# Attention with one shift row, 64-row keys for the maxima, a closing norm on VectorE and output weights loaded two ahead

## The chip, the core and the metric

The kernel runs on one core of a Trainium2 chip. The time is the device time of one execution in microseconds. The engines are TensorE (PE in the profile, its weight loads PEld), VectorE (DVE), ScalarE (ACT), GpSimd (POOL) and SyncE (SP), which here only issues transfers. Each engine takes its instructions in a fixed order and waits at the front of its queue for whatever the next one needs.

## What is computed

One layer on a sequence of 2048 positions of width 1024, cut to its steps:

```python
h = layer_norm(x) * (1 + scale) + shift               # scale, shift, gate = silu(c) @ w_ada + b_ada
xr, zr, q, k, v, za, fl = split(h @ w_in)
y_r = rms_norm(rg_lru(conv(xr))) * silu(zr)           # recurrent half, width 512
d = cumsum(log_sigmoid(fl + b_fgate))                 # one decay per head and position
s = q @ k.T * 64**-0.5 + d[query] - d[key]            # 8 heads of 64, causal
y_a = rms_norm(softmax(s) @ v) * silu(za)             # attention half, width 512
y = concat(y_r, y_a) @ w_out
out = layer_norm(2**0.25 * x + gate * y) * ln_gain + ln_bias
```

Each fp32 operand of the large products is split into a high and a low fp16 part, and a product is three matmuls (high by high, high by low, low by high).

## The kernel before

Up to about 590 us of the span the kernel computes the norm, the projections, the recurrence and the keys, and the sum of the output gate (`gate_gen`, seven GpSimd additions of 1024 columns, line 957). What follows is one long attention stage of 32 units: four query chunks `ci` of 512 positions by eight heads `h`. A unit has two parts.

`maxpass` runs ahead of its unit. It loads the keys `kk` of the head: plane 0 holds the high part in rows 0 to 63 and the low part in rows 64 to 127, from the DRAM tensor `kd`; plane 1 holds the high part again and four further rows, from a second DRAM tensor `kb` of 68 rows (two rows of the constant 1024, two rows with the decay of the keys). It multiplies the high part of the queries `qb` by plane 1 into PSUM (`pmx`, 68 rows), and VectorE takes row maxima (`mc`, line 1259). From the maximum of a query and its decay comes the shift that is subtracted from the scores. Three VectorE instructions on 128x4 elements (lines 1267 to 1269) write it as a high and a low fp16 column into `z`; four small matmuls (`pzt`) transpose `z`, and ScalarE copies two rows into rows 64 and 65 of `qb`.

The unit's steps follow, one for each block of 128 keys. `s_t` makes the scores by two matmuls into `pst`: plane 0 by both parts of the queries (`qs`), and the first 66 rows of plane 1 by `qb`, which brings in the shift. ScalarE takes the exponential (`pf32`) and casts it to the high part (`ph`, line 1292); the low part is a subtraction, on GpSimd for three blocks of four (line 1294) and on VectorE for the fourth (line 1296). `av` follows five steps later and multiplies both parts by the values `V` into `acc`; `fin` divides by the sum and collects the heads in `Y`. The scores, the maxima and the transposes of the shift share five PSUM banks.

Between the steps runs side work, a few yields at a time: the queries of later chunks (`q_side`), the output weights (`wout_gen`) and, from the first finished chunk on, the output (`out_gen`). `wout_gen` loads each of eight weight blocks `woraw` (128x1024) one block ahead, multiplies it by the gate `gbc` on GpSimd (line 1003) right after the load is issued, and splits it. These blocks, the gate, the keys of the first two chunks and the residual tiles `xres` share one pool of eight buffers (`r4`). `out_gen` multiplies each tile of 128 positions by the weights in two halves of 512 columns (48 matmuls), adds the residual `xres` (line 1468), and hands it to `ln_gen`: statistics on VectorE, the reciprocal root `rs` on GpSimd (line 1395), then a small VectorE instruction for `nm`, one ScalarE instruction over 1024 columns (line 1385), and two GpSimd instructions over 1024 columns with the gain and the bias (lines 1387 and 1388). The last tile has a form of its own, `out_last`, with four VectorE instructions of 512 columns (lines 1427 and 1429).

The program is written as generators; the tool that builds it then settles the order on each engine by its own estimate of times. So an edit at one place moves instructions elsewhere as well.

Of the kernel before, what the change touches and what calls it, by code (L numbers as in the profile page):

```python
# [10 lines left out]
F16 = mybir.dt.float16  # L11
# [8 lines left out]
P = 128  # L20
# [18 lines left out]
def hybrid_mixer(  # L39
# [34 lines left out]
    def cst(shape, name, dt=F32):  # L74
        return con.tile(shape, dt, name=name, tag=name)
# [10 lines left out]
    def sm(shape, name, dt=F32):  # L86
        return sb.tile(shape, dt, name=name, tag="sm", bufs=24)
# [15 lines left out]
            tick()  # L103

    kd = dr.tile([H, P, S], F16, name="kd", tag="kd")
    kb = dr.tile([H, 68, S], F16, name="kb", tag="kb")
    vd = dr.tile([S, C], F32, name="vd", tag="vd")
    qd = dr.tile([H, P, S], F16, name="qd", tag="qd")
    zd = dr.tile([4, P, S], F32, name="zd", tag="zd")
# [755 lines left out]
    nc.vector.tensor_scalar(L8p, sp, 8.0, None, ALU.mult)  # L865
    crow = r4([2, S], "crow", F16)
    nc.vector.memset(crow, RS)
    nc.scalar.dma_start(kb[:, DH:DH + 2, :].rearrange("h a s -> a h s"), crow.unsqueeze(1).broadcast_to([2, H, S]))
    QB = [cst([68, CH], f"qb{i}", F16) for i in range(4)]
    Z = [cst([P, 4, 68], f"Z{i}", F16) for i in range(4)]  # L870
    for q in QB:
        nc.scalar.dma_start(q[66:68, :], crow[:, 0:CH])
    for z in Z:
        nc.gpsimd.memset(z, 0.0)

# [7 lines left out]
    def qk_store(dsts, p, hl, sl):  # L883
        for e in range(2):
            es = slice(e * DH, (e + 1) * DH)
            for dst, lo_i, hi_i in dsts:
                nc.sync.dma_start(dst[2 * p + e, hi_i * DH:(hi_i + 1) * DH, sl], hl[es, 0])
                if lo_i is not None:
                    nc.sync.dma_start(dst[2 * p + e, lo_i * DH:(lo_i + 1) * DH, sl], hl[es, 1])

    k_sc = []

    def k_fin(p, u, sts, cols):
        yield
        yield
        am = yield from all_max(col_max(cols))
        inv, rec = sm([P, 1], "ki"), sm([P, 1], "kr")
        scales(am, 4.0, inv, rec)
        f = cst([P, 1], f"fk{p}")
        nc.vector.tensor_tensor(f, u, inv, ALU.mult)  # L900
        k_sc.append(f)
        yield
        for half in range(2):
            hl = wh([P, 2, D], "khl")
            split_out(hl[:, 0], hl[:, 1], sts[half].rearrange("p a b -> p (a b)"), rec)
            qk_store([(kd, 1, 0), (kb, None, 0)], p, hl, slice(half * D, (half + 1) * D))
            yield

    def k_group(p):
# [32 lines left out]
    def gate_gen():  # L942
        for k in range(KT):
            raw = r4([P, D], "woraw")
            nc.sync.dma_start(raw, w_out_v[k])
            nc.vector.tensor_reduce(out=wocol[:, k:k + 1], in_=raw, axis=AX.X, op=ALU.max, apply_absolute_value=True)
            if k % 2 == 1:
                yield
        acc = None
        for k in range(KT):  # L950
            w = r4([P, D], "wgate")
            nc.sync.dma_start(w, w_ada_v[k, :, 2 * D:3 * D])
            nc.scalar.activation(w, w, AF.Copy, scale=cact[:, k:k + 1])
            if acc is None:
                acc = w
            else:
                nc.gpsimd.tensor_tensor(out=acc, in0=acc, in1=w, op=ALU.add)
            if k % 2 == 1:
                yield
        gbc = r4([P, D], "gbc")  # L960
        nc.sync.dma_start(gbc, b_ada[0, 2 * D:3 * D].partition_broadcast(P))
        for n in range(2):
            sl = slice(n * CH, (n + 1) * CH)
            ps = bank("C", "pgt")
            mm(ps, ones, acc[:, sl], True, True)
            nc.vector.tensor_tensor(gbc[:, sl], ps, gbc[:, sl], ALU.add)
        gate["bc"] = gbc
        yield
        cols = sm([P, 2], "amg")
        col_max(g_col, AX.X, cols[:, 0:1])  # L970
        col_max(gbc, AX.X, cols[:, 1:2])
        chains.append(gate_fin(cols))
        yield
# [10 lines left out]
    def wout_gen():  # L984
        gbc = gate["bc"]
        wm = sm([P, KT], "wm")
        nc.vector.tensor_tensor(wm, wocol, mk, ALU.mult)
        col = col_max(wm)
        yield
        yield  # L990
        am = yield from all_max(col)
        am_w = sm([P, 1], "am_w")
        nc.vector.tensor_scalar(am_w, am, TINY, gate["am"], ALU.max, ALU.mult)
        scales(am_w, RS, sc_o[:, 1:2], sc_o[:, 0:1])
        nc.vector.tensor_scalar(kap, sc_o[:, 1:2], 1.0 / YT, None, ALU.mult)
        so = cst([P, KT], "so")
        nc.vector.tensor_tensor(so, g_col, mk, ALU.mult)
        nc.vector.tensor_scalar(so, so, sc_o[:, 0:1], 1.0 / ALPHA, ALU.mult, ALU.mult)
        yield
        def wo_raw(k):  # L1000
            raw = r4([P, D], "woraw")
            nc.sync.dma_start(raw, w_out_v[k])
            nc.gpsimd.tensor_tensor(out=raw, in0=raw, in1=gbc, op=ALU.mult)
            return raw

        nxt = wo_raw(0)
        yield
        for k in range(KT):
            raw = nxt
            if k + 1 < KT:  # L1010
                nxt = wo_raw(k + 1)
            w = wh([P, 2, D], "wo") if k < KT - 1 else r4([P, 2, D], "wo", F16)
            for n in range(2):
                sl = slice(n * CH, (n + 1) * CH)
                split_out(w[:, 0, sl], w[:, 1, sl], raw[:, sl], so[:, k:k + 1])
                yield
            wo.append(w)

# [66 lines left out]
    def decay_gen():  # L1085
# [37 lines left out]
        nc.vector.tensor_tensor(ndr[:, 1], ndf, ndr[:, 0], ALU.subtract)  # L1123
        for h in range(H):
            for a in range(2):
                nc.sync.dma_start(kb[h, DH + 2 + a, :].rearrange("(t p) -> t p", p=P), ndr[h * TT:(h + 1) * TT, a, :])
        yield

    dg = decay_gen()
# [101 lines left out]
    def maxpass(ci, h, res):  # L1231
        n = cnt[0]
        cnt[0] += 1
        qb, z = QB[n % 4], Z[n % 4]
        sl = slice(ci * CH, (ci + 1) * CH)
        nk = (ci + 1) * CH
        if ci < 2:
            kk = r4([P, 2, 2 * CH], "kk", F16)
        else:
            kk = sb.tile([P, 2, S], F16, name="kk", tag="H", bufs=8)  # L1240
        nc.sync.dma_start(kk[:, 0, 0:nk], kd[h, :, 0:nk])
        nc.sync.dma_start(kk[0:68, 1, 0:nk], kb[h, :, 0:nk])
        nc.sync.dma_start(qb[0:DH, :], qd[h, DH:P, sl])
        qs = sb.tile([P, CH], F16, name="qs", tag="qs", bufs=3)
        nc.sync.dma_start(qs, qd[h, :, sl])
        nc.gpsimd.memset(qb[DH:DH + 2, :], 0.0)
        res.append((kk, qb, qs))
        yield
        mc = sm([P, 4, 4], "mc")
        for i in range(4):  # L1250
            nk = (4 * ci + i + 1) * P
            for b in range(ci + 1):
                w = min(CH, nk - b * CH)
# [5 lines left out]
                nc.vector.tensor_reduce(out=mc[:, i, b:b + 1], in_=ps[:, 0:w], axis=AX.X, op=ALU.max)  # L1259
                yield  # L1260
        if ci > 0:
            m = sm([P, 4], "mrow")
            nc.vector.tensor_reduce(out=m, in_=mc[:, :, 0:ci + 1], axis=AX.X, op=ALU.max)
        else:
            m = mc[:, :, 0]
        t = sm([P, 4], "trow")
        nc.vector.tensor_scalar(t, m, -1.0 / RS, ndc[:, ci, h:h + 1], ALU.mult, ALU.add)  # L1267
        nc.vector.tensor_copy(z[:, :, DH], t)  # L1268
        nc.vector.tensor_tensor(z[:, :, DH + 1], t, z[:, :, DH], ALU.subtract)  # L1269
        yield True  # L1270
        yield True
        with tc.issue_after(last["pe"]):
            ps = bank("A", "pzt")
            for i in range(4):
                mm(ps[0:DH + 2, i * P:(i + 1) * P], z[:, i, 0:DH + 2], ident16, i == 0, i == 3, True)
        yield
        nc.scalar.copy(qb[DH:DH + 2, :], ps[DH:DH + 2, :])

    def s_t(ci, h, kt, kk, qb, qs):
        q0 = max(0, kt - 4 * ci) * P  # L1280
# [2 lines left out]
        ps = bank("A", "pst")  # L1283
        mm(ps[:, 0:w], kk[:, 0, ks], qs[:, q0:CH], True, False)
        md = kt >= 4 * ci
        mm(ps[:, 0:w], kk[0:DH + 2, 1, ks], qb[0:DH + 2, q0:CH], False, not md)
        if md:
            mm(ps[:, 0:P], maskn, identb, False, True)
        pf32 = t2([P, CH], "pf32")
# [84 lines left out]
    def ln_gen(tt, xt):  # L1374
# [9 lines left out]
        nc.vector.scalar_tensor_tensor(nm, mv[:, 0:1], -1.0, rs, ALU.mult, ALU.mult)
        nc.scalar.activation(xt, xt, AF.Identity, scale=rs, bias=nm)  # L1385
        yield
        nc.gpsimd.tensor_tensor(out=xt, in0=xt, in1=late["lng"], op=ALU.mult)
        nc.gpsimd.tensor_tensor(out=xt, in0=xt, in1=late["lnb"], op=ALU.add)
# [230 lines left out]
```

## Time and profile before

| quantity | value |
|---|---|
| median of 3 runs | 1217.73 us (1213.55 to 1219.83) |
| profiled execution, time | 1211.64 us |
| its span in the profile | 1209.9 us |
| TensorE busy | 1111.2 us (92%) |
| VectorE / ScalarE / GpSimd busy | 767.7 / 719.6 / 686.0 us |
| mean granted clock of TensorE | 0.966 |

In the profile's views a line names the engine, the source line, the operation and the tiles, with the result left of the arrow. `L93` is the helper that records every matmul, so matmuls are told apart by their tiles. A wait reads "engine line <- what it waited for: us in total, times, longest". In the views by window each engine has busy us and, in brackets, the number of instructions; the granted clock is a share of full speed. "SPq" is the issue of a transfer, not the transfer itself.

### The profile page before, as it was taken

Reading aid. Unit: us, or ns where it says so; the run is one execution under the profiler, and the core shown is the slowest. Engines: PE = TensorE matmul, PEld = TensorE weight load, DVE = VectorE, ACT = ScalarE, POOL = GpSimd, SP = SyncE. Lnnn points to the kernel's source line nnn. Section 1 sums busy time; section 2 is a strip of 40 time slices with the busy share of each in tenths; the row PEclk is TensorE's granted clock in tenths of the full one; section 3 lists DMA queues with packets and bytes.
Section 4 is the critical chain, followed back from the end, with each engine's and each line's share of the span. In section 5 each row is a group of like instructions: output and inputs, shape, how many; then the busy total and the mean of one; then the engine's idle time right before and its main releaser. Section 6 shows DMA issues by size and latency. Waiting matters only on the chain. (4 is left out here: it accounts for less than half of the span.)

```text
span 1209.9 us, 20217 instructions
## 1 busy us (share of the span) xinstructions
PE 1111.2 (92%) x7467; PEld 622.8 (51%) x7467; DVE 767.7 (63%) x1435; ACT 719.6 (59%) x1244; POOL 686.0 (57%) x670
## 2 busy tenths in 40 slices
PE   6997899999999899999979979989999989999787
PEld 6874444454444444434445545555565555565444
DVE  4378775766668953664396544576677677667534
ACT  3437545564758412623375657577888688888841
POOL 5715532444554300830277645687788689887854
PEclk9998989999999999999979989989999999999899
DMA  9653046221225712754063344222332233221001
GB/s 296 208 151 123 1 118 189 71 64 33 70 70 141 242 55 70 260 160 140 26 205 114 95 129 123 87 93 86 101 94 90 76 103 106 78 89 46 18 27 70
DMA packets 110248, 130.56 MB, mean 108 GB/s; under 512 B 10086, under 2 KB 79318, under 8 KB 110150
## 3 DMA queue, kind: packets, MB, share of 16 engines
q1 hardware_dynamic: 109840, 129.17, 35.0%
q8 instruction: 58, 0.95, 0.3%
q14 instruction: 40, 0.33, 0.1%
q10 hardware_dynamic: 310, 0.12, 0.0%
HBM read 97.66 MB, written 31.59 MB: 107 GB/s over the span
## 5 line engine op out<-in xcount | busy, mean ns | idle before, releaser
L93 PE MATMUL pj<-hT,wT 128*128 128x512 f16 x1440 | 324.4, 383 | 4.1 <-DVE hT L347 1.7
L1294 POOL TENSOR_TENSOR ph<-pf,ph 128x512 f16<-128x512 f32 (+2 forms) x240 | 260.5, 1100 | 67.4 <-ACT ph L1292 62.6
L93 PEld LDWEIGHTS <-wT 128*128 128x128 f16 x1792 | 169.2, 99 | 208.6 <-issue 21.6
L1259 DVE TENSOR_REDUCE mc<-pmx 128x1 f32<-128x512 f32 (+2 forms) x320 | 184.8, 603 | 114.2 <-PE pmx L93 110.0
L1290 ACT ACTIVATE pf<-pst,bias 128x512 f32<-128x512 f32 (+1 forms) x320 | 194.7, 634 | 66.4 <-PE pst L93 58.8
L1292 ACT CAST ph<-pf 128x512 f16<-128x512 f32 (+1 forms) x320 | 171.7, 569 | 20.1 <-PE acc L93 15.9
L93 PE MATMUL acc<-V,ph 128*128 128x129 f16 (+1 forms) x2176 | 158.6, 210 | 22.0 <-POOL ph L1294 14.6
L93 PEld LDWEIGHTS <-ph 128*128 128x128 f16 x2176 | 124.1, 99 | 80.6 <-POOL ph L1294 22.1
L93 PE MATMUL pst<-qs,kk 128*128 128x512 f16 (+1 forms) x320 | 114.3, 360 | 2.0 <-DVE mc L1259 1.3
L93 PE MATMUL pst<-qb,kk 66*128 66x512 f16 (+1 forms) x320 | 112.8, 362 | 0.2
L93 PE MATMUL pmx<-kk,qb 68*128 68x512 f16 (+2 forms) x320 | 105.0, 357 | 7.4 <-DMA kk<-kb 3.8
L93 PE MATMUL pout<-wo,yT 128*128 128x512 f16 (+1 forms) x396 | 95.7, 372 | 1.5 <-ACT yT L1370 1.5
L93 PE MATMUL pout<-wo,yr 128*128 128x512 f16 (+1 forms) x396 | 94.1, 381 | 2.8 <-DVE zs L1369 2.7
L93 PE MATMUL pj<-wN,hT 128*128 128x512 f16 x384 | 89.5, 378 | 0.2 <-ACT XL L814 0.2
L1188 POOL TENSOR_TENSOR XL<-XL,szr 128x512 f32<-128x512 f32 x16 | 24.3, 1522 | 114.7 <-ACT szr L1185 114.7
L1296 DVE TENSOR_TENSOR ph<-pf,ph 128x512 f16<-128x512 f32 (+1 forms) x80 | 64.3, 804 | 33.8 <-ACT ph L1292 33.2
L93 PEld LDWEIGHTS <-kk 66*128 66x128 f16 (+1 forms) x640 | 55.1, 100 | 34.5 <-issue 11.6
L93 PE MATMUL pq<-hT,wT 128*128 128x512 f16 x288 | 67.0, 379 | 2.8 <-DVE qhl L881 2.8
L93 PEld LDWEIGHTS <-hT 128*128 128x128 f16 x640 | 44.5, 97 | 48.3 <-issue 3.6
L93 PEld LDWEIGHTS <-yr 128*128 128x128 f16 x396 | 38.3, 100 | 42.8 <-issue 8.0
L93 PEld LDWEIGHTS <-yT 128*128 128x128 f16 x396 | 37.5, 98 | 39.4 <-ACT yT L1370 1.7
L483 POOL TENSOR_TENSOR xl<-xc,xh 128x512 fp32r<-128x512 f32 x16 | 24.4, 1532 | 57.8 <-ACT xh L481 47.0
(307 smaller groups left out, 1846.0 us busy)
## 6 DMA issues: line engine op xcount, KB each, us to landing
wraw<-in_w_in_dram SPq DMA_DIRECT2D x40, 512.0 KB
woraw<-in_w_out_dram SPq DMA_DIRECT2D x16, 512.0 KB
xres<-in_x_dram SPq DMA_DIRECT2D x16, 512.0 KB
out_dram<-xres SPq DMA_DIRECT2D x15, 512.0 KB
wadab<-in_w_ada_dram SPq DMA_DIRECT2D x8, 512.0 KB
xt<-in_x_dram SPq DMA_DIRECT2D x16, 256.0 KB
xt<-in_x_dram SPq DMA_DIRECT2D x8, 512.0 KB
wsh<-in_w_ada_dram SPq DMA_DIRECT2D x16, 256.0 KB
```

Source lines behind the costliest of these rows:

```text
L93: m = nc.tensor.matmul(o, lhsT=l, rhs=r, start=st, stop=sp, skip_group_check=chk)
L483: nc.gpsimd.tensor_tensor(out=xl, in0=xc, in1=xh, op=ALU.subtract)
L1188: nc.gpsimd.tensor_tensor(out=XL[j][:, sl], in0=XL[j][:, sl], in1=sz, op=ALU.mult)
L1259: nc.vector.tensor_reduce(out=mc[:, i, b:b + 1], in_=ps[:, 0:w], axis=AX.X, op=ALU.max)
L1290: nc.scalar.activation(pf32[:, 0:w], ps[:, 0:w], AF.Exp, scale=DH ** -0.5, bias=bias[:, ci, h, kt:kt + 1])
L1292: nc.scalar.copy(ph[:, 0, 0:w], pf32[:, 0:w])
L1294: nc.gpsimd.tensor_tensor(out=ph[:, 1, 0:w], in0=pf32[:, 0:w], in1=ph[:, 0, 0:w], op=ALU.subtract)
L1296: nc.vector.tensor_tensor(ph[:, 1, 0:w], pf32[:, 0:w], ph[:, 0, 0:w], ALU.subtract)
```

## The change

It has four parts. The shift becomes one fp16 column and one row (one VectorE instruction instead of three). The second DRAM copy of the keys' high part goes: plane 1 takes its 64 rows from `kd` again and three rows from a `kb` that holds only one constant row and the two rows of the decay. The gate's sums and the products of the output weights run on GpSimd in halves of 512 columns; the weights are loaded two blocks ahead, and their product is issued a block ahead of the split. The closing norm of the first 15 tiles takes the form of the last one: four VectorE instructions of 512 columns, and none on ScalarE or on GpSimd after `rs`.

```diff
@@ stores and loads of the keys
-    kb = dr.tile([H, 68, S], F16, name="kb", tag="kb")
+    kb = dr.tile([H, 3, S], F16, name="kb", tag="kb")
...
-    nc.scalar.dma_start(kb[:, DH:DH + 2, :].rearrange("h a s -> a h s"), crow.unsqueeze(1).broadcast_to([2, H, S]))
-    QB = [cst([68, CH], f"qb{i}", F16) for i in range(4)]
+    nc.scalar.dma_start(kb[:, 0:1, :].rearrange("h a s -> a h s"), crow[0:1].unsqueeze(1).broadcast_to([1, H, S]))
+    QB = [cst([67, CH], f"qb{i}", F16) for i in range(4)]
...
-        nc.scalar.dma_start(q[66:68, :], crow[:, 0:CH])
+        nc.scalar.dma_start(q[65:67, :], crow[:, 0:CH])
...
-            qk_store([(kd, 1, 0), (kb, None, 0)], p, hl, slice(half * D, (half + 1) * D))
+            qk_store([(kd, 1, 0)], p, hl, slice(half * D, (half + 1) * D))
...
-                nc.sync.dma_start(kb[h, DH + 2 + a, :].rearrange("(t p) -> t p", p=P), ndr[h * TT:(h + 1) * TT, a, :])
+                nc.sync.dma_start(kb[h, 1 + a, :].rearrange("(t p) -> t p", p=P), ndr[h * TT:(h + 1) * TT, a, :])
...
         nc.sync.dma_start(kk[:, 0, 0:nk], kd[h, :, 0:nk])
-        nc.sync.dma_start(kk[0:68, 1, 0:nk], kb[h, :, 0:nk])
+        nc.sync.dma_start(kk[0:DH, 1, 0:nk], kd[h, 0:DH, 0:nk])
+        nc.sync.dma_start(kk[DH:DH + 3, 1, 0:nk], kb[h, :, 0:nk])
@@ sum of the gate
-                nc.gpsimd.tensor_tensor(out=acc, in0=acc, in1=w, op=ALU.add)
+                for n in range(2):
+                    sl = slice(n * CH, (n + 1) * CH)
+                    nc.gpsimd.tensor_tensor(out=acc[:, sl], in0=acc[:, sl], in1=w[:, sl], op=ALU.add)
@@ output weights
         def wo_raw(k):
             raw = r4([P, D], "woraw")
             nc.sync.dma_start(raw, w_out_v[k])
-            nc.gpsimd.tensor_tensor(out=raw, in0=raw, in1=gbc, op=ALU.mult)
             return raw
 
-        nxt = wo_raw(0)
-        yield
+        def wo_gate(raw):
+            for n in range(2):
+                sl = slice(n * CH, (n + 1) * CH)
+                nc.gpsimd.tensor_tensor(out=raw[:, sl], in0=raw[:, sl], in1=gbc[:, sl], op=ALU.mult)
+
+        raws = [wo_raw(0), wo_raw(1)]
+        yield
+        wo_gate(raws[0])
         for k in range(KT):
-            raw = nxt
-            if k + 1 < KT:
-                nxt = wo_raw(k + 1)
+            raw = raws.pop(0)
             w = wh([P, 2, D], "wo") if k < KT - 1 else r4([P, 2, D], "wo", F16)
             for n in range(2):
                 sl = slice(n * CH, (n + 1) * CH)
                 split_out(w[:, 0, sl], w[:, 1, sl], raw[:, sl], so[:, k:k + 1])
+                if n == 0 and k + 2 < KT:
+                    raws.append(wo_raw(k + 2))
+                if n == 0 and k + 1 < KT:
+                    wo_gate(raws[0])
                 yield
@@ maxima and shift
-        nc.gpsimd.memset(qb[DH:DH + 2, :], 0.0)
+        nc.gpsimd.memset(qb[DH:DH + 1, :], 0.0)
...
-                mm(ps[:, 0:w], qb[:, i * P:(i + 1) * P], kk[0:68, 1, b * CH:b * CH + w], True, not end)
+                mm(ps[:, 0:w], qb[:, i * P:(i + 1) * P], kk[0:67, 1, b * CH:b * CH + w], True, not end)
...
-        t = sm([P, 4], "trow")
-        nc.vector.tensor_scalar(t, m, -1.0 / RS, ndc[:, ci, h:h + 1], ALU.mult, ALU.add)
-        nc.vector.tensor_copy(z[:, :, DH], t)
-        nc.vector.tensor_tensor(z[:, :, DH + 1], t, z[:, :, DH], ALU.subtract)
+        nc.vector.tensor_scalar(z[:, :, DH], m, -1.0 / RS, ndc[:, ci, h:h + 1], ALU.mult, ALU.add)
...
-                mm(ps[0:DH + 2, i * P:(i + 1) * P], z[:, i, 0:DH + 2], ident16, i == 0, i == 3, True)
-        yield
-        nc.scalar.copy(qb[DH:DH + 2, :], ps[DH:DH + 2, :])
+                mm(ps[0:DH + 1, i * P:(i + 1) * P], z[:, i, 0:DH + 1], ident16, i == 0, i == 3, True)
+        yield
+        nc.scalar.copy(qb[DH:DH + 1, :], ps[DH:DH + 1, :])
...
-        mm(ps[:, 0:w], kk[0:DH + 2, 1, ks], qb[0:DH + 2, q0:CH], False, not md)
+        mm(ps[:, 0:w], kk[0:DH + 1, 1, ks], qb[0:DH + 1, q0:CH], False, not md)
@@ closing norm, ln_gen
-        nm = sm([P, 1], "nm")
-        nc.vector.scalar_tensor_tensor(nm, mv[:, 0:1], -1.0, rs, ALU.mult, ALU.mult)
-        nc.scalar.activation(xt, xt, AF.Identity, scale=rs, bias=nm)
-        yield
-        nc.gpsimd.tensor_tensor(out=xt, in0=xt, in1=late["lng"], op=ALU.mult)
-        nc.gpsimd.tensor_tensor(out=xt, in0=xt, in1=late["lnb"], op=ALU.add)
+        for n in range(2):
+            ns = slice(n * CH, (n + 1) * CH)
+            nc.vector.scalar_tensor_tensor(xt[:, ns], xt[:, ns], mv[:, 0:1], late["lng"][:, ns], ALU.subtract, ALU.mult)
+            yield
+        for n in range(2):
+            ns = slice(n * CH, (n + 1) * CH)
+            nc.vector.scalar_tensor_tensor(xt[:, ns], xt[:, ns], rs, late["lnb"][:, ns], ALU.mult, ALU.add)
+            if n == 0:
+                yield
```

The order on the engines moves as follows. SP, where the last of the eight weight blocks is loaded (`kk` are keys, `yr` the recurrent half, `qd` the stored queries); before:

```order
L1242 DMA kk_6507<-kb_64 68x1024
L1245 DMA qs_6511<-qd_66 128x512
L1243 DMA qb0_1604<-qd_66 64x512
L1241 DMA kk_7814<-kd_63 128x1536
L887 DMA qd_66<-qhl_6548 64x512 x2
L889 DMA qd_66<-qhl_6548 64x512 x2
L1242 DMA kk_7814<-kb_64 68x1536
L1241 DMA kk_8101<-kd_63 128x1536
L1242 DMA kk_8101<-kb_64 68x1536
L1326 DMA yr_8216<-yd_68 128x2x512 x4
L1245 DMA qs_6784<-qd_66 128x512
L1002 DMA woraw_6555<-in_w_out_dram 128x1024
```

and now:

```order
L887 DMA qd_66<-qhl_6369 64x512
L888 DMA qd_66<-qhl_6369 64x512
L1003 DMA woraw_6379<-in_w_out_dram 128x1024
L1252 DMA qb0_1604<-qd_66 64x512
L1249 DMA kk_6485<-kd_63 128x1024
L1250 DMA kk_6485<-kd_63 64x1024
L1251 DMA kk_6485<-kb_64 3x1024
L1249 DMA kk_7780<-kd_63 128x1536
L1250 DMA kk_7780<-kd_63 64x1536
L1251 DMA kk_7780<-kb_64 3x1536
```

The last `woraw` stood behind the key loads of two later units and the four of `yr`; now it stands ahead of them, and a key load has three rows.

GpSimd at the product of this block (`ph` the low part of the probabilities, `ytmp` and `Y` the collection of a finished head); before:

```order
L1294 TENSOR_TENSOR ph_6533<-pf32_6531,ph_6533 128x512
L1316 TENSOR_TENSOR ytmp_6633<-ytmp_6633 128x2x64
L1294 TENSOR_TENSOR ph_6566<-pf32_6564,ph_6566 128x512
L1317 TENSOR_TENSOR Y_6236<-ytmp_6633,rv_6635 128x2x64
L1294 TENSOR_TENSOR ph_6622<-pf32_6620,ph_6622 128x512
L1294 TENSOR_TENSOR ph_6654<-pf32_6652,ph_6654 128x384
L1246 MEMSET qb1_1605 2x512
L1003 TENSOR_TENSOR woraw_6555<-woraw_6555,gbc_4622 128x1024
L1294 TENSOR_TENSOR ph_6694<-pf32_6692,ph_6694 128x256
```

and now:

```order
L1300 TENSOR_TENSOR ph_6474<-pf32_6472,ph_6474 128x512
L1009 TENSOR_TENSOR woraw_6379<-woraw_6379,gbc_4613 128x512 x2
L1322 TENSOR_TENSOR ytmp_6605<-ytmp_6605 128x2x64
L1322 TENSOR_TENSOR ytmp_6611<-ytmp_6611 128x2x64
L1340 TENSOR_TENSOR yrst_6497<-yss_6366,mhalf_91 128x4
L1323 TENSOR_TENSOR Y_6216<-ytmp_6605,rv_6607 128x2x64
L1323 TENSOR_TENSOR Y_6216<-ytmp_6611,rv_6613 128x2x64
L1300 TENSOR_TENSOR ph_6512<-pf32_6510,ph_6512 128x512
L1300 TENSOR_TENSOR ph_6544<-pf32_6542,ph_6544 128x512
L1300 TENSOR_TENSOR ph_6600<-pf32_6598,ph_6600 128x512
```

The product came after the subtractions that are now named ph_6512 to ph_6632; it now comes ahead of them, as two halves.

VectorE at the shift of one unit; before:

```order
L1296 TENSOR_TENSOR ph_9833<-pf32_9831,ph_9833 128x512
L1263 TENSOR_REDUCE mrow_9868<-mc_9662 128x4
L1267 TENSOR_SCALAR trow_9870<-mrow_9868,ndc_3534 128x4
L1268 CAST Z2_1610<-trow_9870 128x4
L1269 TENSOR_TENSOR Z2_1610<-trow_9870,Z2_1610 128x4
L1259 TENSOR_REDUCE mc_9968<-pmx_9969 128x1
```

and now:

```order
L1302 TENSOR_TENSOR ph_9782<-pf32_9780,ph_9782 128x512
L1272 TENSOR_REDUCE mrow_9817<-mc_9612 128x4
L1275 TENSOR_SCALAR Z2_1610<-mrow_9817,ndc_3522 128x4
L1477 SCALAR_TENSOR_TENSOR xres_9054<-pout_9751,kap_1622,xres_9054 128x512
L1384 BN_STATS bst_9692<-xres_9054 128x6
```

Two of the three small instructions are gone, and the transfer needs only the one that is left.

VectorE a little further on, at the closing norm of a tile; before:

```order
L1380 BN_AGGR mv_10003<-bst_9743 128x2
L1296 TENSOR_TENSOR ph_9932<-pf32_9930,ph_9932 128x128
L1393 TENSOR_SCALAR ve_10005<-mv_10003 128x1
L1314 RECIPROCAL rv_10064<-ytmp_10062 128x2
L1259 TENSOR_REDUCE mc_9968<-pmx_9988 128x1
L1259 TENSOR_REDUCE mc_9968<-pmx_9991 128x1
L1468 SCALAR_TENSOR_TENSOR xres_9609<-pout_10045,kap_1622,xres_9609 128x512
L1259 TENSOR_REDUCE mc_9968<-pmx_10023 128x1
L1259 TENSOR_REDUCE mc_9968<-pmx_10038 128x1
L1314 RECIPROCAL rv_10070<-ytmp_10068 128x2
L1259 TENSOR_REDUCE mc_9968<-pmx_10041 128x1
L1384 SCALAR_TENSOR_TENSOR nm_10123<-mv_10003,rs_10007 128x1
```

and now:

```order
L1268 TENSOR_REDUCE mc_9917<-pmx_9918 128x1
L1386 BN_AGGR mv_9952<-bst_9692 128x2
L1302 TENSOR_TENSOR ph_9880<-pf32_9878,ph_9880 128x128
L1402 TENSOR_SCALAR ve_9954<-mv_9952 128x1
L1391 SCALAR_TENSOR_TENSOR xres_9054<-xres_9054,mv_9952,lng_7040 128x512 x2
L1395 SCALAR_TENSOR_TENSOR xres_9054<-xres_9054,rs_9956,lnb_7042 128x512 x2
L1268 TENSOR_REDUCE mc_9917<-pmx_9937 128x1
L1268 TENSOR_REDUCE mc_9917<-pmx_9940 128x1
```

Where one small `nm` came nine instructions behind `ve`, four instructions of 512 columns now follow `ve` directly, the last two of them behind `rs` from GpSimd; the maxima `mc` of the next unit stand behind them.

More of the change, by code (lines that the diff above doesn't have):

```diff
@@ L887, in qk_store @@
                 nc.sync.dma_start(dst[2 * p + e, hi_i * DH:(hi_i + 1) * DH, sl], hl[es, 0])
-                if lo_i is not None:
-                    nc.sync.dma_start(dst[2 * p + e, lo_i * DH:(lo_i + 1) * DH, sl], hl[es, 1])
+                nc.sync.dma_start(dst[2 * p + e, lo_i * DH:(lo_i + 1) * DH, sl], hl[es, 1])
     k_sc = []
```

## The prediction

> **What bounds the kernel now.** I read the engine shares of the page first, then busy time by stage, then the waits of the attention stage, and last the places where TensorE stands longest.
>
> The share of TensorE over the span:
>
> ```profile
> PE 1111.2 (92%) x7467; PEld 622.8 (51%) x7467; DVE 767.7 (63%) x1435; ACT 719.6 (59%) x1244; POOL 686.0 (57%) x670
> ```
>
> TensorE is the bound. The change takes no matmul away, so it can only shorten the 99 us in which TensorE is idle (1209.9 - 1111.2) and the stretches in which its clock is lowered. By stage (columns: length; busy us and instructions of PE, PEld, DVE, ACT, POOL; granted clock; DMA share; GB/s):
>
> ```profile
> 590.00:800.00 210.00, 184.62 (x1451) 106.91 (x1449) 129.79 (x286) 140.20 (x288) 136.12 (x163) 0.94 0.40 118
> 800.00:1000.00 200.00, 187.91 (x1600) 109.07 (x1601) 140.34 (x264) 153.28 (x299) 154.84 (x163) 0.96 0.29 92
> 1000.00:1160.00 160.00, 149.55 (x1373) 89.63 (x1371) 103.43 (x184) 132.43 (x253) 135.65 (x130) 0.97 0.19 65
> 1160.00:1210.00 50.00, 40.99 (x220) 21.52 (x218) 19.48 (x40) 9.30 (x13) 22.30 (x15) 0.95 0.14 52
> ```
>
> The edits lie almost wholly in these four stages, which hold 57 us of the idle time (620 - 563.1). From 800 to 1160 ScalarE (286 of 360 us) and GpSimd (290) are fuller than VectorE (244). What TensorE and the two others wait for between 590 and 1210 us (total us, times, longest):
>
> ```profile
> PE acc L93 <- POOL ph L1294: 14.6, 20, 3.5
> PE pzt L93 <- DVE Z L1269: 9.1, 10, 2.3
> ...
> PE pmx L93 <- DMA kk<-kb: 3.8, 3, 1.5
> ...
> PE pmx L93 <- DVE mc L1259: 2.3, 4, 1.6
> ...
> PE pst L93 <- DVE mc L1259: 1.3, 4, 0.7
> ```
>
> ```profile
> DVE mc L1259 <- PE pmx L93: 108.0, 90, 7.6
> ```
>
> ```profile
> POOL ph L1294 <- ACT ph L1292: 62.6, 45, 8.9
> ...
> POOL woraw L1003 <- DMA woraw<-in_w_out_dram: 14.3, 5, 7.6
> ```
>
> Two waits of TensorE are aimed at by the change: for the small parts of the probabilities (GpSimd), and for the shift (VectorE). VectorE itself mostly waits for TensorE, so it has room.
>
> **Output weights two ahead.** Eight 512 KB loads keep their number; each is now issued two blocks early, and the multiply by the gate one block early, in halves. The worst place before:
>
> ```profile
> 679.62 0.54 SPq L1241 DMA_DIRECT2D kk<-kd  x1
> ...
> 696.38 1.49 SPq L1002 DMA_DIRECT2D woraw<-in_w_out_dram  x1
> ...
> 704.27 2.34 POOL L1003 TENSOR_TENSOR woraw<-woraw,gbc 128x1024 f32<-128x1024 f32 x1 [7.65 <-DMA woraw<-in_w_out_dram]
> ```
>
> ```profile
> 700.00:710.00 10.00, 4.83 (x28) 2.36 (x27) 2.61 (x3) 4.49 (x10) 5.73 (x5) 0.84 0.36 109
> 710.00:720.00 10.00, 9.06 (x46) 4.77 (x46) 7.27 (x13) 5.68 (x11) 5.51 (x7) 0.65 0.39 126
> ```
>
> GpSimd stood 7.65 us before a multiply whose weights had been asked for 7.9 us earlier, and the probabilities queued behind it. In these 20 us TensorE was idle 5.17 + 0.94 = 6.1 us, and at the lowered clock it lost at most 1.6 + 3.5 = 5.1 us more (slice times one minus the clock). So the gain is 11.2 us at most. In the new order this load stands on SP ahead of the keys that were issued from 679.62 on, so some 17 us sooner, while its multiply stands only four subtractions sooner on GpSimd. The other end is a loss: three raw blocks instead of two share eight buffers with the keys, and late keys already cost the 3.8 us of the waits above. I take -8, nearer the gain, because the load gets 17 us of lead and the multiply gives back only some 5 (four subtractions of 1.1 us, whose row stands below).
>
> **Shift as one row.** Per unit (32 of them) three instructions on VectorE become one; the transfer matmuls and the copy keep their number:
>
> ```profile
> L1267 DVE TENSOR_SCALAR trow<-mrow,ndc 128x4 f32<-128x4 f32 x24 | 14.7, 614 | 0.7
> L1268 DVE CAST Z<-trow 128x4 f16<-128x4 f32 x32 | 14.5, 454 | 0.5
> L1269 DVE TENSOR_TENSOR Z<-trow,Z 128x4 f16<-128x4 f32 x32 | 18.4, 574 | 0.9
> ```
>
> ```profile
> L1267 DVE TENSOR_SCALAR trow<-mrow,ndc x24: 219/530/1174, 652.3 to 1128.6; 128x4 f32<-128x4 f32 x24
> L1268 DVE CAST Z<-trow x32: 164/178/1134, 590.3 to 1129.8; 128x4 f16<-128x4 f32 x32
> ```
>
> The new instruction is not in the trace. It has the arithmetic of L1267 and the output of L1268, so it lies between 164 and 1174 ns; I take L1267's 614, its nearest relative. VectorE saves 32 x (454 + 574) = 32.9 us. On the path this counts only where the transfer waits, at most 9.1 us. Why four columns can take 2 us:
>
> ```profile
> 936.96 2.36 POOL L1388 TENSOR_TENSOR xres<-xres,lnb 128x1024 f32<-128x1024 f32 x1
> 937.08 2.27 DVE L1269 TENSOR_TENSOR Z<-trow,Z 128x4 f16<-128x4 f32 x1
> 939.41 0.64 PE L93 MATMUL pzt<-ident,Z 128*66 128x128 f16 x4 [1.64 <-DVE Z L1269]
> ```
>
> The little subtraction ends when GpSimd's 1024-column addition ends, and TensorE stands behind it. Of 1.64 us a unit (614 + 454 + 574) 63% goes, so 63% of 9.1 is 5.7; I take -5, ends 0 and -9.1. After such waits the clock falls:
>
> ```profile
> 800.00:810.00 10.00, 8.65 (x46) 4.63 (x47) 7.64 (x12) 7.01 (x14) 9.12 (x10) 0.62 0.32 111
> 810.00:820.00 10.00, 10.00 (x63) 4.93 (x62) 3.62 (x7) 6.73 (x15) 4.97 (x5) 0.87 0.11 43
> ```
>
> That is at most 3.8 + 1.3 = 5.1 us at this one place, and other units have smaller ones; I take -4 for all of them, ends 0 and -10. [...]
>
> **Closing norm.** Fifteen tiles; what goes, and what comes from the last tile, which already has the new form:
>
> ```profile
> L1387 POOL TENSOR_TENSOR xres<-xres,lng 128x1024 f32<-128x1024 f32 x15 | 35.4, 2357 | 9.6 <-ACT xres L1385 9.2 <-PE pmx L93 0.4
> L1388 POOL TENSOR_TENSOR xres<-xres,lnb 128x1024 f32<-128x1024 f32 x15 | 35.3, 2352 | 0.3
> L1385 ACT ACTIVATE xres<-xres,nm,rs 128x1024 f32<-128x1024 f32 x15 | 18.8, 1251 | 16.8 <-DVE nm L1384 16.7
> ```
>
> ```profile
> L1427 DVE SCALAR_TENSOR_TENSOR xres<-xres,mv,lng x2: 745/746/748, 1204.3 to 1204.9; 128x512 f32<-128x512 f32 x2
> L1384 DVE SCALAR_TENSOR_TENSOR nm<-mv,rs x15: 141/159/881, 761.5 to 1195.1; 128x1 f32<-128x1 f32 x15
> ```
>
> GpSimd loses 70.7 us and ScalarE 18.8. VectorE gains 60 x 0.746 = 44.8 and loses 15 x 0.159 = 2.4; with the 32.9 above it ends 9.5 us fuller, before any waiting. GpSimd's 70.7 us are 16% of its 448.9 us from 590 on; 16% of TensorE's 14.6 us wait for it is 2.3, and all of it 14.6. I take -4, above the proportional share, since these are its longest instructions and the probabilities queue behind them. The cost is what VectorE now does while GpSimd works:
>
> ```profile
> 803.55 2.34 POOL L1388 TENSOR_TENSOR xres<-xres,lnb 128x1024 f32<-128x1024 f32 x1
> 803.63 2.41 DVE L1296 TENSOR_TENSOR ph<-pf,ph 128x128 f16<-128x128 f32 x1
> ```
>
> ```profile
> L1294 POOL TENSOR_TENSOR ph<-pf,ph 128x512 f16<-128x512 f32 (+2 forms) x240 | 260.5, 1100 | 67.4 <-ACT ph L1292 62.6 <-PE pmx L93 2.4 <-POOL ph L1294 0.2
> L1395 POOL TENSOR_TENSOR rs<-ve,mhalf 128x1 f32<-128x1 f32 x16 | 9.7, 603 | 11.7 <-DVE ve L1393 11.7
> ```
>
> A VectorE instruction with two SBUF inputs waited out a GpSimd one. So each new one takes 0.746 us alone and up to 0.746 + 1.10 behind a subtraction: 3.0 to 7.4 us a tile, in which the maxima, the zs of the next tile and VectorE's quarter of the probabilities queue. The second pair also waits for rs from GpSimd: 0.6 us, with a subtraction ahead of it 1.7. VectorE's idle time from 800 to 1160 is 116 us, so it has room on the average; what counts is how late the maxima get. I take 0.4 us of TensorE a tile, +6, between 0 and 3 us a tile (+45), nearer 0 because its waits for maxima are now 2.3 + 1.3 us in all (rows above) though VectorE is held 2.4 us at a time.
>
> [...]
>
> **The rest.** Each unit loads its keys with three transfers instead of two, and sixteen stores of the high halves go: 16 more issues on SP. The first maxima wait for one more landing; +1, ends 0 and +3.8 (the wait quoted above). Fewer rows cost a matmul nothing:
>
> ```profile
> L93 PE MATMUL pst<-qs,kk 128*128 128x512 f16 (+1 forms) x320 | 114.3, 360 | 2.0 <-DVE mc L1259 1.3
> L93 PE MATMUL pst<-qb,kk 66*128 66x512 f16 (+1 forms) x320 | 112.8, 362 | 0.2
> ```
>
> The gate's seven sums become fourteen halves, before 590 us and under full matmuls: 0. In the tail TensorE runs output matmuls without a break:
>
> ```profile
> 1171.32 15.54 PE pout L93 x72
> ```
>
> A tile needs 48 of these, 10.4 us. VectorE is busy 19.5 of the last 50 us and gets 3.0 us more a tile: 0.
>
> **Sum.** -8 - 5 - 4 - 4 + 6 + 1 = -14 us. The profiled execution took 1211.64 us, so 1197.6; the median of the runs, 1217.73, stands 6.1 us above it, and 1217.73 - 14 gives 1204.
>
> **Rivals.** (1) Slower: VectorE, held by GpSimd in the four norm instructions, delays the maxima until the banks of the scores are full. The other terms make -20, so it decides from 20 / 15 = 1.3 us of TensorE a tile; at 2 us, +30 instead of +6, the time is 1228. For it: the row of 803 us. Against: 116 us of idle VectorE. (2) No change: the waits pass on. GpSimd already waits 62.6 us for ScalarE's casts, so a freer GpSimd may only wait longer; norm and clock terms 0, the shift half, gives -8 - 2.5 + 6 + 1 = -3.5 and 1214. (3) All that is aimed at goes: -11.2 - 9.1 - 10 - 4 + 6 + 1 = -27 and 1190.
>
> **Chances.** Forecast 0.45, (3) 0.18, (2) 0.21, (1) 0.16. About 0.5%, 6.1 us, is what a measurement of this kernel can tell from no change, so faster 0.63, same 0.21, slower 0.16. The range runs from 1187, just below (3), to 1224, between (2) and (1); for the forecast alone 1197 to 1211.
>
> **What would show it.** Weights: no wait of GpSimd for them above 2 us, and TensorE over 9 of 10 us busy where it was 4.83. Shift: its wait under 4 us in all. Norm: GpSimd near 615 us, VectorE near 777 plus its holds, the new instructions at 0.75 to 1.9 us. Wrong would be waits of matmuls for maxima in place of these, or the key loads late behind the weights.

## The result, and the profile after

The changed kernel takes 1201.36 us (median of 4 runs, 1197.99 to 1202.03), the kernel before, on the same chip, 1216.48 (4 runs): a ratio of 0.9869, 95% interval 0.9836 to 0.9902, or 16 us less of about 1217. The profiled execution took 1201.11 us with a span of 1199.3. The direction and the size are those of the forecast (1204). The terms behind it are not: the weights cost 6 us where a gain of 8 was taken, and the keys gain 3.6 us alone and 10 beside the shift where a loss of 1 was taken.

The shares of the engines over the span, and the four stages of the attention part (same columns as before):

```profile
PE 1107.4 (92%) x7467; PEld 622.2 (52%) x7467; DVE 776.1 (65%) x1416; ACT 705.0 (59%) x1229; POOL 629.7 (53%) x655
```

```profile
590.00:800.00 210.00, 191.26 (x1491) 110.67 (x1490) 124.17 (x263) 140.59 (x289) 135.89 (x170) 0.93 0.41 120
800.00:1000.00 200.00, 188.94 (x1656) 111.64 (x1655) 149.25 (x270) 154.81 (x306) 143.37 (x157) 0.98 0.33 100
1000.00:1150.00 150.00, 140.08 (x1297) 83.58 (x1296) 100.79 (x176) 120.32 (x234) 106.43 (x114) 0.98 0.18 57
1150.00:1199.00 49.00, 40.81 (x220) 21.59 (x218) 27.39 (x48) 5.07 (x8) 9.53 (x9) 0.97 0.13 49
```

From 590 to 800 TensorE is busy 6.6 us more than before and so further on in its work, at a slightly lower clock; from 800 to 1000 the clock is 0.98 instead of 0.96. What TensorE waits for from 590 us on (total, times, longest):

```profile
PE acc L93 <- POOL ph L1300: 10.0, 21, 1.6
PE pmx L93 <- DMA kk<-kd: 9.1, 3, 6.0
...
PE pmx L93 <- DVE mc L1268: 3.3, 4, 2.3
PE pzt L93 <- DVE Z L1275: 2.9, 2, 1.9
PE pst L93 <- DVE mc L1268: 2.5, 5, 0.8
```

The wait for the shift fell from 9.1 to 2.9 us, that for GpSimd's probabilities from 14.6 to 10.0 with a longest of 1.6 instead of 3.5. But the wait for keys, 3.8 us before with a longest of 1.5, is 9.1 us now, one of them 6.0. It lies here:

```profile
680.00:690.00 10.00, 5.10 (x39) 2.56 (x36) 0.84 (x2) 3.92 (x11) 6.89 (x8) 0.86 0.36 108
690.00:700.00 10.00, 8.42 (x30) 3.73 (x31) 4.31 (x10) 4.18 (x7) 3.06 (x4) 0.63 0.53 147
700.00:710.00 10.00, 10.00 (x87) 5.94 (x86) 5.92 (x10) 8.47 (x17) 3.23 (x4) 1.00 0.63 180
```

The slice of 700 us, 4.83 busy before, is full, and a slice of 5.10 has come up 20 us ahead of it. The timeline around it (start, length, engine, line; in brackets the idle time ahead and what ended it):

```profile
681.08 0.53 SPq L1003 DMA_DIRECT2D woraw<-in_w_out_dram  x1
...
685.46 2.48 POOL L1009 TENSOR_TENSOR woraw<-woraw,gbc 128x512 f32<-128x512 f32 x2 [0.44 <-DMA woraw<-in_w_out_dram]
...
687.96 0.33 SPq L1249 DMA_DIRECT2D kk<-kd  x1
```

```profile
691.58 0.59 PE L93 MATMUL pmx<-kk,qb 67*128 67x512 f16 x1 [6.05 <-DMA kk<-kd]
```

```profile
SPq L1249 <- POOL woraw L1009: 5.8, 1, 5.8
```

The last row is from the waits of SP's queue: the issue of a key load stood 5.8 us, until the product of the last weight block was done on GpSimd, and TensorE stood 6.05 us behind it. A stall for weights had become a stall for keys. The other long one of the key waits, 2.8 us at 769 us, is not at the weights: two of the kernels below with weights one block ahead have it too (2.6 and 3.1 us near 760 us).

The groups of the new instructions (total us, mean ns of one):

```profile
L1395 DVE SCALAR_TENSOR_TENSOR xres<-xres,rs,lnb 128x512 f32<-128x512 f32 x30 | 33.8, 1154 | 0.4 <-POOL rs L1404 0.4
L1391 DVE SCALAR_TENSOR_TENSOR xres<-xres,mv,lng 128x512 f32<-128x512 f32 x30 | 26.7, 928 | 0.0
L1275 DVE TENSOR_SCALAR Z<-mrow,ndc 128x4 f16<-128x4 f32 x24 | 9.1, 378 | 0.5
```

### The profile page after: what moved, and what is told of

Same layout as the page of the kernel before. It is cut to its first block, busy times and chain, and to the rows that moved or that the text cites. A ratio compares the mean times of both kernels' runs of the same rounds, so it can differ in the third digit from the quotient of the medians.

```text
span 1199.3 us, 20226 instructions
## 1 busy us (share of the span) xinstructions
PE 1107.4 (92%) x7467; PEld 622.2 (52%) x7467; DVE 776.1 (65%) x1416; ACT 705.0 (59%) x1229; POOL 629.7 (53%) x655
## 5 line engine op out<-in xcount | busy, mean ns | idle before, releaser
L1300 POOL TENSOR_TENSOR ph<-pf,ph 128x512 f16<-128x512 f32 (+2 forms) x240 | 267.6, 1128 | 98.5 <-ACT ph L1298 87.7
L93 PE MATMUL pmx<-kk,qb 67*128 67x512 f16 (+2 forms) x320 | 104.8, 361 | 14.0 <-DMA kk<-kd 9.1
L93 PE MATMUL pst<-qb,kk 65*128 65x512 f16 (+1 forms) x320 | 111.6, 357 | 0.1
L93 PE MATMUL pout<-wo,yr 128*128 128x512 f16 (+1 forms) x396 | 91.4, 375 | 1.4 <-DVE zs L1375 1.3
L1196 POOL TENSOR_TENSOR XL<-XL,szr 128x512 f32<-128x512 f32 x16 | 21.9, 1369 | 120.1 <-ACT szr L1193 120.1
L1302 DVE TENSOR_TENSOR ph<-pf,ph 128x512 f16<-128x512 f32 (+1 forms) x80 | 58.2, 728 | 39.3 <-ACT ph L1298 38.2
L93 PEld LDWEIGHTS <-kk 65*128 65x128 f16 (+1 forms) x640 | 54.7, 100 | 31.5 <-issue 9.0
L93 PEld LDWEIGHTS <-hT 128*128 128x128 f16 x640 | 44.4, 97 | 48.4 <-issue 3.8
L93 PE MATMUL pj<-h,w 128*128 128x512 f32 x192 | 51.7, 421 | 3.1 <-ACT h L380 3.1
```

The costliest lines, as they stand in the source:

```text
L93: m = nc.tensor.matmul(o, lhsT=l, rhs=r, start=st, stop=sp, skip_group_check=chk)
L1196: nc.gpsimd.tensor_tensor(out=XL[j][:, sl], in0=XL[j][:, sl], in1=sz, op=ALU.mult)
L1300: nc.gpsimd.tensor_tensor(out=ph[:, 1, 0:w], in0=pf32[:, 0:w], in1=ph[:, 0, 0:w], op=ALU.subtract)
L1302: nc.vector.tensor_tensor(ph[:, 1, 0:w], pf32[:, 0:w], ph[:, 0, 0:w], ALU.subtract)
```

## The experiments

Twelve kernels are made from the kernel before or from the changed one, with one part put in, left out or altered. Each was timed in five rounds beside the kernel before, and the ratio is against that kernel on the same chip; 0.001 is 1.2 us. The kernels of a group were timed together, and so were the first three of the last group.

### Each part alone

Weights and gate: only `wo_raw`, `wo_gate` and the halves, as in the diff.

> The kernel before with one part of the change alone: gate sums and weight products in halves, weights two ahead. Theory A (the parts add up as in the prediction): -8 us beside the kernel before (bounds -11.2 and +4), the stretch around 707 us back above 9 of 10 us busy, GpSimd's wait for the weights under 6 us. Theory B (the weights' wait only changes its name): the loads put ahead on SP delay the keys, so that TensorE stands 4 to 7 us once for a key load near 690 us, as in the changed kernel, and the part gives -4 to 0 us. Theory C (a new order of the whole stage makes the difference): anything between -6 and +6 us with gaps at places that have nothing to do with the weights.

Measured: 1231.5 us, ratio 1.0116 (1.0083 to 1.0149): 14 us slower. The wait for the weights' block near 707 us is gone, and a wait of 7.0 us for a key load stands at 703 us. Theory B has the place; the loss is larger than any of the three said.

Closing norm: only the four VectorE instructions in `ln_gen`.

> The kernel before with the closing norm of the first 15 tiles on VectorE alone. Theory A: GpSimd near 615 us, ScalarE 19 us less, and a time between -4 and +2 us beside the kernel before (the prediction's terms -4 and +6, and some of the -4 for the clock). Theory B (GpSimd's long instructions were what held the shift and the probabilities): TensorE's wait for the shift falls from 9.1 to under 4 us and for GpSimd's probabilities from 14.6 to under 10, and the part gives -8 to -5 us with the shift's three instructions still there. Rival (VectorE is held by GpSimd): waits of matmuls for maxima rise above 10 us in all, +5 us or more.

Measured: 1220.34 us, ratio 1.0018 (0.9993 to 1.0043): no change that can be told. GpSimd is busy 631.8 us, but TensorE's waits for the shift (9.9 us) and for GpSimd's probabilities (13.5) are what they were. So theory A, with the time just past the end of its range (2.2 us); theory B falls, and so does the rival, which asked for more than 10 us of waits for maxima: they are 4.7 + 1.7 us.

Shift, with a second copy of the keys that has 67 rows:

```diff
-    kb = dr.tile([H, 68, S], F16, name="kb", tag="kb")
+    kb = dr.tile([H, 67, S], F16, name="kb", tag="kb")
-        nc.sync.dma_start(kk[0:68, 1, 0:nk], kb[h, :, 0:nk])
+        nc.sync.dma_start(kk[0:67, 1, 0:nk], kb[h, :, 0:nk])
...
+        nc.vector.tensor_scalar(z[:, :, DH], m, -1.0 / RS, ndc[:, ci, h:h + 1], ALU.mult, ALU.add)
```

> The kernel before with the shift as one fp16 row alone; the keys of the maxima still come from a second DRAM copy, in one transfer of 67 rows. Theory A: VectorE loses some 30 us, TensorE's wait for the shift falls from 9.1 to about 4 us, and the time is -5 to -9 us beside the kernel before (shift -5, its share of the clock up to -4). Theory B (the wait is GpSimd's long additions, not the number of instructions): the one instruction left still waits out a 1024-column addition, the shift's wait stays above 6 us and the part gives -2 to 0 us.

Measured: 1268.34 us, ratio 1.0424 (1.0394 to 1.0453): 51 us slower, which neither theory had. The shift's wait fell to 3.3 us as theory A has it. But VectorE and TensorE now wait for transfers of all kinds (`zs` is a tile of the attention half's gate, loaded from DRAM):

```profile
PE pout L93 <- DVE zs L1366: 30.6, 6, 13.5
PE acc L93 <- POOL ph L1291: 21.9, 16, 13.2
PE pmx L93 <- DMA kk<-kb: 16.1, 3, 5.7
```

```profile
DVE zs L1366 <- DMA zs<-zd: 28.6, 4, 14.0
```

The view of the DMA engines says why. First this kernel in the ten microseconds from 1061 on, then the kernel before in 1.6 us at the end of a transfer of 68 rows of its last unit:

```profile
DMA packets 65, 0.26 MB, mean 26 GB/s; under 512 B 1, under 2 KB 1, under 8 KB 65
```

```profile
DMA packets 42, 0.17 MB, mean 105 GB/s; under 512 B 2, under 2 KB 2, under 8 KB 41
```

For ten microseconds hardly anything moves but packets of 4 KB, 64 of them, one each 0.156 us: 67 rows (0.268 MB) one behind the other would be 67 x 0.156 = 10.5 us, an estimate. With 68 rows the tail moves at four times that rate: by the same estimate 68 / 4 x 0.156 = 2.7 us. In the same two views the queue's packets take 6.4% of the time of the 16 engines, as much as one of them has, and 25.6%, as much as four. A later load stood behind the tail of 67 rows: a `zs` asked for at 1057.23 us was read by VectorE at 1072.75, after a wait of 14.0 us. Why one row less changes the rate so, no run here shows.

Keys: plane 1 from `kd` and a `kb` of four rows, everything else as before.

> The kernel before with the second DRAM copy of the keys dropped alone: four rows kept, three key transfers a unit instead of two, sixteen stores less. Theory A: +1 us beside the kernel before (0 to +3.8), waits of matmuls for keys between 3.8 and 7 us in all. Theory B (the third transfer is what makes the keys late in the changed kernel): a wait for a key load of 4 us or more near 690 us, +3 to +6 us.

Measured: 1211.75 us, ratio 0.9970 (0.9946 to 0.9993): 3.6 us faster, against both theories. TensorE's wait for keys fell from 3.8 to 0.9 us. The third transfer costs nothing that is seen; the tail of the 68 rows is what the edit takes out of the attention stage. It also drops the sixteen stores, but those lie ahead of it, and up to 590 us TensorE is as busy as before (549 and 548 us).

### Parts together and left out

Shift as one row, with the 68-row transfer as it was (only the four edits of `z`, the transposes, the copy and the second score matmul):

> The kernel before with the shift as one fp16 row, and the key transfer of 68 rows left as it is (the second row of the shift stays zero). Theory R (rows per transfer: in the run of the shift with 67 rows the tail of each such transfer moved 4096-byte packets one after the other at 23 to 35 GB/s, so those 67 rows were what cost 50 us): the loss goes, no transfer has a one-at-a-time tail, and the shift alone gives -9 to 0 us beside the kernel before. Rival S (the new order of the program that one instruction instead of three brings was what cost it): still +20 us or more, with the same stalls of 5 to 14 us for weights, keys and zs.

Measured: 1201.86 us, ratio 0.9905 (0.9879 to 0.9930): 11.5 us faster. Theory R holds, with a gain somewhat above its range. One row less in each transfer (1.0424 against 0.9905, from two chips) costs 63 us.

Shift and keys as in the changed kernel, with the old weights and the old norm:

> The changed kernel with the old weights code and the old closing norm: shift as one row and keys by 64 + 3 rows together. Theory R: both gains come together, -4 us for the keys (measured alone) and -5 for the shift: 1204 to 1212 us. Rival O (every edit deals the order anew and the parts do not add): outside of 1200 to 1216.

Measured: 1191.74 us, ratio 0.9827 (0.9796 to 0.9858): 21 us faster, beyond both ends of what theory R expected. By its number this is rival O: the parts do not add. Beside the shift alone, on the same chip, the keys are worth another 10.1 us (1201.86 to 1191.74).

The changed kernel without its weights part:

> The changed kernel with the old weights code (one block ahead, whole blocks). Theory W (loading two ahead pays, as predicted -8 us): 1205 to 1213 us, TensorE again standing 4 us or more for probabilities behind a late weight block. Rival V (loading two ahead costs by late keys, +14 us alone): 1185 to 1197 us, no wait for a key load above 3 us near 690 us. Rival O (no part has a price of its own): 1199 to 1204.

Measured: 1190.87 us, ratio 0.9820 (0.9788 to 0.9852): theory V. Without the weights part the kernel is faster by 6.0 us (0.9869 - 0.9820 of 1217, from two chips), though the old wait for a late weight block is back, 2.9 us at 701 us.

The changed kernel with the old norm:

> The changed kernel with the old closing norm (ScalarE and two GpSimd instructions of 1024 columns). Theory A (GpSimd freed pays 4 us, VectorE's holds cost 6; +2 us measured alone): within 4 us of the changed kernel. Theory G (with the other parts in place the long GpSimd instructions are what would hold the queue again): 1207 to 1215 us, TensorE's wait for the shift or for GpSimd's probabilities up by 5 us or more.

Measured: 1198.11 us, ratio 0.9865 (0.9834 to 0.9896): as the changed kernel, theory A. TensorE's waits for the shift (2.7) and for GpSimd (8.2) stay low with the long GpSimd instructions in place, so it was not the freed GpSimd that took them down. The wait for the shift falls with the shift as one row alone (3.1 us in that run). The wait for GpSimd's probabilities does not (15.2 there, 13.4 with the keys); beside shift and keys it falls with the weights part (13.4 to 8.2), though that part loses more elsewhere. Beside shift and keys alone, on the same chip, the weights cost 6.4 us here (1191.74 to 1198.11).

### What in the weights part costs

One block ahead, products still in halves:

```diff
-        raws = [wo_raw(0), wo_raw(1)]
+        raws = [wo_raw(0)]
...
-                if n == 0 and k + 2 < KT:
-                    raws.append(wo_raw(k + 2))
                 if n == 0 and k + 1 < KT:
+                    raws.append(wo_raw(k + 1))
                     wo_gate(raws[0])
```

> The changed kernel with the weights loaded one block ahead again, the products still in halves and still issued ahead of the next split. Theory T (the third block in flight is what costs 6 us: it takes a buffer of the shared eight, and a key load then waits for the last product): as without the weights part, 1187 to 1195 us, no wait for a key load above 4 us near 690 us, the old wait for a late weight block near 700 us back. Rival H (the halves on GpSimd cost it): 1197 to 1204 us, as the changed kernel.

Measured: 1192.0 us, ratio 0.9790 (0.9748 to 0.9833): theory T. TensorE again stands 3.3 us for probabilities behind the late weight block at 700 us, and 1.1 us for keys.

Two blocks ahead, gate sums and products in whole blocks:

> The changed kernel with the weights two blocks ahead, but gate sums and products in whole blocks of 1024 columns again. Theory T: as the changed kernel, 1197 to 1204 us, with the wait of about 6 us for a key load near 690 us. Rival H: 1187 to 1195 us.

Measured: 1198.89 us, ratio 0.9848 (0.9804 to 0.9892): theory T again, 6.9 us above the one before on the same chip. The stall is there, with the same wait on SP's queue, in this order the waits of TensorE and those of SP:

```profile
PE pmx L93 <- DMA kk<-kb: 8.0, 2, 5.3
```

```profile
SPq L1245 <- POOL woraw L1005: 5.4, 1, 5.4
```

One VectorE instruction more, with no work in it:

```diff
+    dum = sm([P, 1], "dum")
+    nc.vector.memset(dum, 0.0)
     mg = maxpass(*items[0], res)
```

> The kernel before with one VectorE memset of a single column more, ahead of the attention stage: no work to speak of, but a new occasion for the order to be dealt. If the order alone moves the time of this kernel by as much as the small parts did (2 to 6 us), it shows here: outside of 0.997 to 1.003. If not, the parts of 0.3% and more are the parts' own: within 2 us of the kernel before.

Measured: 1218.28 us, ratio 1.0015 (0.9988 to 1.0042). This one new occasion for the order to be dealt moves the time by no more than the measurement can tell; other occasions were not tried. Taken as the scale for the others: the shift, the keys beside the shift and the weights stand clear of it, the norm does not, and the keys alone (0.9970) hardly do.

A ninth buffer in the pool `r4` (memory taken from the small tiles), everything else as in the changed kernel:

```diff
-        return sb.tile(shape, dt, name=name, tag="r4", bufs=8)
+        return sb.tile(shape, dt, name=name, tag="r4", bufs=9)
...
-        return sb.tile(shape, dt, name=name, tag="t2", bufs=10)
+        return sb.tile(shape, dt, name=name, tag="t2", bufs=8)
```

> The changed kernel (weights two ahead, in halves) with nine buffers in the shared pool instead of eight; the memory for the ninth comes from the pool of the small tiles, eight instead of ten. Theory P (the key load near 690 us waits for a buffer of the pool, which the third weight block has taken): no wait of TensorE above 2 us for a key load near 690 us and no weight wait near 700 us either; 1186 to 1196 us, unless the two small tiles less cost something elsewhere, which the waits would show. Rival Q (the key is late because it stands behind the weight load in the queue, whatever buffers there are): the wait of about 6 us stays, 1197 us or more.

Measured: 1184.18 us (1182.23 to 1188.55), ratio 0.9764 (0.9723 to 0.9805): the fastest kernel here, 1% ahead of the changed one. Theory P by its time and by TensorE's waits; rival Q falls. The stretch where both kernels had stood:

```profile
680.00:690.00 10.00, 10.00 (x70) 5.35 (x69) 6.34 (x14) 7.29 (x15) 8.10 (x11) 1.00 0.65 170
690.00:700.00 10.00, 10.00 (x91) 5.93 (x90) 3.89 (x8) 8.12 (x17) 5.76 (x8) 1.00 0.92 253
700.00:710.00 10.00, 10.00 (x83) 5.79 (x81) 6.39 (x14) 5.98 (x13) 4.50 (x6) 1.00 0.55 161
```

TensorE is full at full clock, and from 590 to 800 us no matmul waits for a key load any more; those for GpSimd's probabilities are 1.3 us in all, with 3.0 in the changed kernel. The key load that stands behind the last product is still there, though, 20 us sooner: the last block is asked for at 661.17 us instead of 681.08, and this load goes out as its product ends.

```profile
665.07 2.49 POOL L1009 TENSOR_TENSOR woraw<-woraw,gbc 128x512 f32<-128x512 f32 x2 [0.50 <-issue]
667.59 0.33 SPq L1249 DMA_DIRECT2D kk<-kd  x1
```

```profile
SPq L1249 <- POOL Y L1323: 3.0, 1, 3.0
```

The view puts this wait down to the next GpSimd instruction, which starts at 667.52 and ends only after the issue; at 3.0 us, that early, it holds up no matmul. So with nine buffers the loss is gone, and what the trace shows of it is the earlier last block rather than a key load that no longer waits. Whether the third block in flight then pays is open. Beside one block ahead the ratios are 0.9764 and 0.9790, from different chips and with overlapping intervals, and the key wait of 2.6 us that one block ahead has near 760 us is gone here as well, in a place without weights. Nine buffers with one block ahead were not run. Which buffer the key load waits for follows from the kernel's text: the last product is the last reader of `gbc`, while the block itself is still read by the split. A gate with a buffer of its own was not run either.

## Why the prediction was right in the sum and wrong in the terms

**Shift: -5, and most of -4 for the clock.** Right in kind, a little small. Alone it is worth 11.5 us (8.5 to 14.7); -9 for both terms lies inside. The wait went from 9.1 to 2.9 us (5.7 was taken of it), and the instruction left takes 378 ns on the average (24 of the 32); 614 was taken, from the one that wrote fp32. With the shift alone the clock from 800 to 1000 us is 1.00 instead of 0.96, at most 8 us in that stage; over whole runs on the same chip its median goes from 0.966 to 0.969, at most 3.6 us, so the 4 that were taken are about right. The mean of the changed kernel is 0.966 as before; its new stall costs clock again (0.63 from 690 to 700 us). Ahead of the slice of 800 us the one long gap was 2.3 us, up to 800.95; the clock was 1.00 until 802 us and 0.50 from 804 on. In the changed kernel the mean of 0.86 from 680 to 690 us, with 0.50 from 690 to 696, puts the start of half clock near 687.2 us (an estimate), 1.7 us into the gap of 6.05 that began at 685.53.

**Loads: +1, ends 0 and +3.8.** Wrong in sign: -3.6 alone and -10.1 beside the shift. The step that failed is "16 more issues on SP", which priced a transfer by its issue. What the runs show is a price by rows: 68 end in a tail of some 2.7 us at 105 GB/s (the estimate above), 67 in one of some 10 us at 26 GB/s, with VectorE standing 14.0 us for a load behind it. Of the waits that were quoted for this term (3.8 us for `kk<-kb`) 2.9 went with that tail; they had been read as a price of late keys in general. Why keys and shift together give 21 us, where alone they give 11.5 and 3.6, no run settles. Part of it is clock: beside the shift the keys raise its median from 0.969 to 0.974, at most 6 of the 10.1 us.

**Weights: -8, ends -11.2 and +4.** Wrong: +6.0 (from two chips), +6.4 and +6.9 in three pairs, and +14 alone. The step that failed is the choice "nearer the gain". The loss was named, three blocks and the keys on eight buffers, but was bounded by the 3.8 us of waits that the old arrangement showed. The profile of the kernel before had a row that tells more, in the waits of SP's queue:

```profile
SPq L1241 <- POOL woraw L1003: 4.4, 1, 4.4
```

There too a key load stands until the last product is done, and goes out at 706.63 us. It is the fifth load of 1024 columns, and it cost TensorE 1.2 us at 710.94. In the changed kernel the last block is asked for ahead of the fourth such load, whose keys TensorE needs next, so the fourth gets the place behind the product. One block ahead, with the halves, it is the fifth again (4.5 us on SP's queue, 1.1 us of TensorE). So the wait was not new; what the prediction missed is which load would stand in it. Its bound should have been a whole load, from its issue to the end of the product, 681.08 to 687.94 us here. What the part aimed at was there, too: with the ninth buffer the stretch is full. Alone, with the 68-row transfers still there, the part costs 14 us; the key wait of 7.0 us is half of that, the median clock falls from 0.963 to 0.958, at most 6 us more, and the rest is not traced.

**Closing norm: -4 on GpSimd, +6 for holds.** Right as a pair: +2.2 alone, -0.9 beside shift and keys, +0.5 within the changed kernel, none told from zero. The holds are real. With GpSimd idle the second pair of a tile took 1.40 us (at 1174.27 and 1185.06 us), beside GpSimd's subtractions 3.30 (at 1111.80). At 0.74 us each, the median of the first pair, the 60 instructions would take 44.4 us; they take 60.5 (26.7 + 33.8), so VectorE is held 16.1 us, 1.1 a tile, while TensorE's waits for maxima grew only from 3.6 to 5.8 us. Rival (1) needed 1.3 us of TensorE a tile; the part alone leaves 0.15 net of what it gains (2.2 / 15), and 0.35 at the end of its interval.

**Signs that were named.** Shift under 4 us: 2.9. VectorE near 777 plus its holds, which makes 793: 776.1, since the shift's instruction takes 11.9 us in all where 19.6 were taken, and VectorE's quarter of the subtractions 58.2 instead of 64.3. GpSimd near 615: 629.7, since its subtractions take 267.6 us instead of 260.5, the reciprocal roots `rs` 15.4 instead of 9.7 and the products in halves 20.9 instead of 19.4. The longer subtractions and `rs` point to holds of GpSimd by VectorE as well: `rs` took 0.97 to 1.01 us beside the first pair and 0.54 at 883.75, just behind it. No wait for weights above 2 us: wrong, 4.0 is the longest. TensorE over 9 of 10 at 700 us: right at the place, but the stall had only moved. "Key loads late behind the weights" stood among the signs of error, and that is what came.

**The sum.** 21 us off for shift and keys, 0.9 for the norm, 6.0 back for the weights: 16, as measured. The forecast had 8 off for shift, clock and loads, 2 on for the norm and 8 off for the weights: 14. That the two agree to 2 us is luck: the gain that was missed and the loss that was missed are of one size. In one table, with the ratios to the kernel before:

| kernel | ratio | us of 1217 |
|---|---|---|
| shift (68 rows) | 0.9905 | -11.5 |
| shift and keys | 0.9827 | -21 |
| shift, keys, norm | 0.9820 | -22 |
| shift, keys, weights | 0.9865 | -16 |
| all four (the change) | 0.9869 | -16 |
| all four, nine buffers | 0.9764 | -29 |

## What to carry to other kernels

Look at the number of rows of every transfer: it can cost more than the bytes. Here 64 + 3 rows in two transfers beat 68 in one by 10.1 us beside the shift, and 67 in one cost 63 us more than 68. A load issued earlier holds a buffer longer; before it is moved ahead, read the waits of the issuing queue and ask which load gets the next buffer of that pool, since a load that waits for one holds every load behind it in its queue (5.8 us here). When a change has parts, time them apart and together: this one was 16 us faster with one part in it that cost 6, and with a ninth buffer that part's stall was gone.

## What the runs showed of the hardware that was not expected

A transfer of 67 rows of 4 KB moved at 26 GB/s at its end, 6.4% of the time of 16 engines and by estimate some 10 us for 268 KB, where 68 rows moved at 105 GB/s and 25.6%; one row less took the kernel with the shift from 0.9905 to 1.0424 of the time before. And 16 us in which VectorE was held beside GpSimd (3.30 us for a pair that took 1.40 with GpSimd idle) came with 2.2 us more of TensorE's waits for maxima; what covered the rest is not shown.
